# Row factors, low parts and attention's row sums moved from GpSimd to VectorE, and a longer written order in an MLP, in a two-layer decoder trunk

## The chip, the cores and the metric

The kernel runs on one core of a Trainium2 chip. A core has a matrix engine (TensorE, PE in the profile), a vector engine (VectorE, DVE), an engine for activation functions (ScalarE, ACT), a general engine (GpSimd, POOL) and a queue that issues transfers (SyncE, SP). They run side by side, each through its own list of instructions in order, and wait for each other by semaphores. The metric is the device time of one execution in microseconds; the median over the runs counts.

## The reference

A residual stream h of 1024 positions by 1024 channels, in float32, passes two layers. Each layer is a token mixer, an MLP and a gated embedding:

```python
h = h + rmsnorm(mixer(rmsnorm(h, g_mix_pre)), g_mix_post)
f = square(relu(rmsnorm(h, g_ffn_pre) @ w_up)) @ w_down          # 1024 -> 4096 -> 1024
h = h + rmsnorm(f, g_ffn_post)
e = sigmoid(rmsnorm(h, g_ple_pre) @ w_gate + b_gate) * (p[i] @ w_proj)
h = h + rmsnorm(e, g_ple_post)
```

with rmsnorm(x, g) = x * (mean(x^2) + 1e-6)^-0.5 * g. The first layer's mixer is a gated MLP over chunks of 128 positions. The second's is differential attention with eight heads: each head has two causal softmaxes over scores of width 64, and its rows are (softmax 1 - lambda * softmax 2) times values of width 128, followed by an RMS norm per head and an output projection.

## The kernel before

**Numbers in two parts.** A float32 operand is split into a high part, a copy rounded by ACT, and a low part, the difference, made by DVE or POOL. A product then takes three matmuls: high by high, high by low, low by high. `split` (line 111) does this for weights, line 114 being the subtraction; its argument `eng` says which engine subtracts. `WStream` loads blocks of weights in a written sequence and passes `nc.gpsimd` for those that were added with `pool=True`. `cut` is the same for activations.

**Tiles.** The 1024 positions are eight tiles (tt = 0 to 7) of 128 rows, with 1024 columns each. An RMS norm of a tile needs a factor per row: ACT squares the tile and sums each row, and `rstd_of` (line 240) makes the factor of it on POOL in two operations on a 128x1 column, a multiply-add (line 243) and a power with exponent -0.5 (line 244). After a mixer, an MLP or an embedding there is a post-norm: the row sum comes in two halves, DVE adds them (line 401 in `post_part`, line 838 in `whole`), `rstd_of` follows, then `residual` (line 344) adds the scaled tile to h, stores it, and where a product follows, `pre_norm` squares it again (328), makes a second factor with `rstd_of`, and scales it (330). `transpose_to` then queues transposes on PE (296) and the cut of the result (282, 283) for a moment that is counted in columns of matmuls. Eight tiles have their factors at the start and in the gated MLP's layer norm, eight tiles pass five pre-norms and six post-norms: 104 calls of `rstd_of`.

**Order.** The whole program is emitted in one sequence. PE keeps that sequence throughout. The other engines' order is set by a planner, from estimated durations and from what is ready, except inside a block marked as manual for them, where the instructions emitted inside keep their order among themselves; other instructions may still be put between these.

**The MLP's second product** has four groups (g = 0 to 3) of 16, 16, 16 and 8 steps, numbered m = 0 to 55. A step is 24 matmuls. `after(m)` loads operands of later steps (`load_down`, by the list `lead_l`), stores what earlier splits left over (`store`), and splits operands of steps two or three ahead (`split_down`, by `lead_s`; lines 528 and 771 to 772). At a group's last step `evict` adds the PSUM banks into the tiles (lines 824 to 826 for the third group). Behind the third group, tiles 0 to 3 are done and have their post-norm, residual and pre-norm while the fourth group runs; the weights of the gate (lines 119 and 120) and, by `resident`, the four operands of the embedding's projection are loaded and split meanwhile. A manual block for PE, SP, ACT and DVE begins ahead of step 0 and ends where m reaches `FREE` = 45, that is three steps ahead of the third group's end.

**Attention** runs over sixteen units: heads 0 to 7 with the first 512 rows, then heads 0 to 7 with the last 512. A unit has eight scores: two softmaxes times four row tiles. For each, PE makes the scores, DVE the row maximum (1138), ACT the exponential (1141). After the second softmax of a row tile t, DVE makes a factor (1145, 1146), and the two are combined in A. For t = 1 and 3 one fused operation does this on DVE (line 1149). For t = 0 and 2 the second softmax is scaled in place, by DVE (1152) or ACT (1154), and added by POOL (1155). Some scores later PE transposes A (1167), ACT and DVE cut it (1171, 1172), PE multiplies by the values (1179 to 1181); `norm` and `close` finish the head, and `close` splits the result, its low part being POOL's (line 1208). Between all this PE works on projections that are handed to it piece by piece (`FILL`): the rest of the values, and the output projection, whose weights `w_o` are loaded and split three times in four blocks, the first two times with POOL (line 114).

## Time and profile before

| what | value |
|---|---|
| median of 3 runs | 2371.8 us (2368.11 to 2376.4) |
| the profiled execution | 2373.36 us |
| its span, first to last instruction | 2371.7 us |
| PE busy | 2316.4 us, 98% |
| DVE busy | 1603.4 us, 68% |
| ACT busy | 1167.3 us, 49% |
| POOL busy | 235.7 us, 10%, 303 instructions |
| granted TensorE clock | 0.994 |

The profile lists for one execution what each engine did and when. A row of a group of instructions has the line of the code, the engine, the operation, the tiles written and read, the shapes and the count; behind the bar the time in which any of them ran, in us, the mean of one in ns, and the idle time of the engine just before them with what ended it. A row of the timeline begins with the start and the duration in us; the brackets hold the idle time before it and what it waited for. A row of busy times has the stretch, its length, then each engine's busy time with its count of instructions, the granted clock, and the share and rate of the transfers. PEld is the weight load, which runs beside PE. Matmuls overlap, so PE's single durations add up to more than its busy time.

### The profile page before, as it was taken

The page shows a single profiled execution, that of the slowest core. Times are in us where ns is not written, and L with a number is a line of the kernel's source. Part 1 is how long each engine was busy: PE and PEld are TensorE (multiplying, and loading weights), DVE is VectorE, ACT ScalarE, POOL GpSimd, SP SyncE. Part 2 cuts the span into 40 slices and gives each one's busy share as a digit, 9 for nine tenths or more (in the row PEclk, how much of TensorE's full clock was granted, in tenths as well). Part 3 has the DMA queues.
Part 4 walks back from the last instruction along what each step waited for, and adds up shares of the span by engine and source line. Part 5 has one row for each costly group of instructions (what it writes and reads, how often), then busy time and mean ns, then how long its engine had stood idle before and what let it go on. Part 6 is the DMA issues. An engine that isn't in the chain of part 4 may idle for free.

```text
span 2371.7 us, 30563 instructions
## 1 busy us (share of the span) xinstructions
PE 2316.4 (98%) x10748; PEld 1919.4 (81%) x10748; DVE 1603.4 (68%) x2492; ACT 1167.3 (49%) x2003; POOL 235.7 (10%) x303
## 2 busy tenths in 40 slices
PE   9999999999999998999999989999999999999898
PEld 7888888888888877888887878777888888887787
DVE  4733697777856965563435888878877785876654
ACT  6232575555533446462324766657555553544541
POOL 1100100000000022010001342321000000000410
PEclk9999999999999999999999999999999999999999
DMA  9111445445888975154445765554544577988433
GB/s 334 57 36 54 150 157 183 160 158 189 287 255 297 292 243 213 63 180 145 162 134 181 222 189 138 160 187 138 191 159 161 175 282 240 294 287 298 159 107 125
DMA packets 205035, 441.04 MB, mean 186 GB/s; under 512 B 21552, under 2 KB 56368, under 8 KB 204752
## 3 DMA queue, kind: packets, MB, share of 16 engines
q1 hardware_dynamic: 204448, 437.89, 55.5%
q8 instruction: 85, 1.39, 0.3%
q0 software_dynamic: 432, 1.19, 0.2%
q14 instruction: 70, 0.57, 0.1%
HBM read 310.02 MB, written 133.17 MB: 187 GB/s over the span
## 4 chain that ended last, share of the span: by engine, by line
PE 64%; DVE 4%; DMA 3%; ACT 2%; POOL 1%; issue 1%; SPq 0%; DVEq 0%; POOLq 0%; ACTq 0%
PE pm_c L356 5%; PE pm_c L357 5%; PE pm_c L358 5%; PE pb L368 5%; PE pb L357 4%; PE pm_a L368 4%; PE pb L356 4%; PE pb L358 4%; PE pm_a L356 4%; PE pm_a L357 4%; PE pm_a L358 4%; PE pm_c L368 3%; PE pt L357 2%; PE pt L356 2%; PE pt L358 2%; DMA raw<-in_w_o_dram 1%
## 5 line engine op out<-in xcount | busy, mean ns | idle before, releaser
L368 PE MATMUL pm_a<-w,xh 128*128 128x512 f32 x704 | 222.4, 394 | 2.7 <-ACT w L119 1.8
L368 PEld LDWEIGHTS pm_a<-w,xh 128*128 128x128 f32 x704 | 131.0, 188 | 30.4 <-ACT w L119 3.0
L368 PE MATMUL pb<-w,xh 128*128 128x512 f32 x416 | 135.6, 402 | 5.5 <-DVE gbc L1027 2.9
L527 ACT ACTIVATE w<-ma 128x512 fp32r<-128x512 f32 x130 | 82.3, 635 | 114.2 <-PE pm_a L357 40.4
L368 PE MATMUL pm_a<-w,xl 128*128 128x512 f32 x352 | 138.2, 393 | 0.0
L114 POOL TENSOR_TENSOR s<-s 128x1024 fp32r<-128x1024 f32 x8 | 19.8, 2486 | 1131.5 <-ACT s L113 570.3
L527 ACT ACTIVATE xh<-xl 128x1024 fp32r<-128x1024 f32 x72 | 75.2, 1053 | 80.4 <-DMA xl<-hid 71.4
L528 DVE TENSOR_TENSOR xl<-xl,xh 128x1024 fp32r<-128x1024 f32 x72 | 87.5, 1219 | 28.1 <-ACT xh L527 27.8
L357 PE MATMUL pm_a<-xl,w 128*128 128x512 f32 x260 | 101.3, 390 | 0.2 <-DVE xl L283 0.2
L356 PE MATMUL pm_a<-xh,w 128*128 128x512 f32 x260 | 101.4, 390 | 0.0
L358 PE MATMUL pm_a<-xh,w 128*128 128x512 f32 x260 | 101.2, 389 | 0.0
L243 POOL TENSOR_SCALAR small<-small 128x1 f32<-128x1 f32 x104 | 43.1, 414 | 530.1 <-DVE small L401 322.8
L368 PEld LDWEIGHTS pb<-w,xh 128*128 128x128 f32 x416 | 77.5, 191 | 20.1 <-DVE xn L398 3.4
L528 DVE TENSOR_TENSOR w<-ma,w 128x512 fp32r<-128x512 f32 x130 | 88.5, 682 | 0.0
L527 ACT ACTIVATE s<-s 128x1024 fp32r<-128x1024 f32 x56 | 58.8, 1053 | 54.9 <-DMA s<-hid 38.2
L368 PE MATMUL pb<-w,xl 128*128 128x512 f32 x208 | 83.4, 401 | 0.0
L528 DVE TENSOR_TENSOR s<-s 128x1024 fp32r<-128x1024 f32 x56 | 68.1, 1220 | 22.0 <-ACT s L527 21.8
L344 DVE SCALAR_TENSOR_TENSOR hin<-ma,small,hin 128x1024 f32<-128x1024 f32 (+1 forms) x45 | 56.5, 1257 | 37.6 <-DMA hin<-h 22.8
L356 PE MATMUL pb<-xh,w 128*128 128x512 f32 x204 | 79.7, 391 | 0.0
L358 PE MATMUL pb<-xh,w 128*128 128x512 f32 x204 | 79.4, 389 | 0.0
L357 PE MATMUL pb<-xl,w 128*128 128x512 f32 x204 | 79.4, 389 | 0.0
L368 PEld LDWEIGHTS pm_a<-w,xl 128*128 128x128 f32 x352 | 66.2, 188 | 12.9
(510 smaller groups left out, 7013.8 us busy)
## 6 DMA issues: line engine op xcount, KB each, us to landing
xl<-hid SPq DMA_DIRECT2D x56, 512.0 KB, 4.7
ma<-in_f_w_up_dram SPq DMA_DIRECT2D x48, 512.0 KB, 3.7
ma<-in_f_w_down_dram SPq DMA_DIRECT2D x92, 256.0 KB, 5.2
hid<-ma SPq DMA_DIRECT2D x80, 256.0 KB, 2.4
s<-hid SPq DMA_DIRECT2D x40, 512.0 KB, 5.1
h<-hin SPq DMA_DIRECT2D x36, 512.0 KB, 3.2
hin<-h SPq DMA_DIRECT2D x36, 512.0 KB, 4.2
hid<-xn SPq DMA_DIRECT2D x64, 256.0 KB, 2.5
```

Source lines behind the costliest of these rows:

```text
L114: (eng or nc.vector).tensor_tensor(out=lo, in0=raw, in1=f32(hi), op=ALU.subtract)
L243: nc.gpsimd.tensor_scalar(out=ss, in0=ss, scalar1=1.0 / n, scalar2=eps, op0=ALU.mult, op1=ALU.add)
L344: nc.vector.scalar_tensor_tensor(out=h[:, cs], in0=t_ap[:, cs], scalar=rs, in1=h[:, cs], op0=ALU.mult, op1=ALU.add)
L356: nc.tensor.matmul(ps, lhsT=lh, rhs=rh, start=start, stop=False)
L357: nc.tensor.matmul(ps, lhsT=lh, rhs=rl, start=False, stop=False)
L358: nc.tensor.matmul(ps, lhsT=ll, rhs=rh, start=False, stop=stop)
L368: nc.tensor.matmul(ps, lhsT=xs(l, kc, tt * P), rhs=r[:, cs], start=kc == 0 and k == 0, stop=kc == KC - 1 and k == 2)
L527: act(h, v, AF.Copy)
L528: vec(out=l, in0=v, in1=f32(h), op=sub)
```

## The change

For post-norms, ACT's Square takes the scale 1/32, so that the row sums come out divided by 1024. DVE's addition of the two halves becomes a fused one that adds epsilon as well, and POOL does the power alone (`post_rstd`). Pre-norms, the start and the layer norm keep both POOL operations. The low parts of the embedding's four operands, of w_o's first two passes and of each head's result are made by DVE. Attention's rows are combined by the fused DVE operation for all four row tiles; the scaling by DVE or ACT and POOL's addition go. In the MLP's second product the manual block ends at step 47, behind the third group's evictions and ahead of the post-norms, not ahead of step 45; and `after` no longer calls `store` a second time from step 45 on.

```diff
     def rstd_of(ss, n, eps):
-        k = ss.shape[1]
         nc.gpsimd.tensor_scalar(out=ss, in0=ss, scalar1=1.0 / n, scalar2=eps, op0=ALU.mult, op1=ALU.add)
-        nc.gpsimd.tensor_tensor(out=ss, in0=ss, in1=mhalf[:, :k], op=ALU.pow)
+        root_of(ss)
+
+    def root_of(x):
+        nc.gpsimd.tensor_tensor(out=x, in0=x, in1=mhalf[:, 0:1], op=ALU.pow)
+
+    ROOT = 1.0 / 32
+
+    def post_rstd(s):
+        nc.vector.scalar_tensor_tensor(out=s[:, 0:1], in0=s[:, 0:1], scalar=RMS_EPS, in1=s[:, 1:2],
+                                       op0=ALU.add, op1=ALU.add)
+        root_of(s[:, 0:1])
...
-        nc.scalar.activation(junk, src, AF.Square, accum_out=ssq[tt][:, cb:cb + 1])
+        nc.scalar.activation(junk, src, AF.Square, scale=ROOT, accum_out=ssq[tt][:, cb:cb + 1])
...
-            s = ssq[tt]
-            nc.vector.tensor_tensor(out=s[:, 0:1], in0=s[:, 0:1], in1=s[:, 1:2], op=ALU.add)
-            rstd_of(s[:, 0:1], D, RMS_EPS)
+            post_rstd(ssq[tt])
...
-        split(nc, f32(lo), hi, lo, eng=nc.gpsimd)
+        split(nc, f32(lo), hi, lo)
...
-        FREE = 3 * NQ - 3
...
-            if t >= FREE:
-                store()
...
         for m, (g, c) in enumerate(steps):
-            if m == FREE:
-                strict.__exit__(None, None, None)
...
             if c == n_c - 1 and g == 2:
+                strict.__exit__(None, None, None)
                 for p in range(4):
                     half(p, 1)
...
-                if t in STT[u.hf]:
-                    nc.vector.scalar_tensor_tensor(out=a_, in0=e, scalar=f, in1=a_, op0=ALU.mult, op1=ALU.add)
-                else:
-                    if t in TS[u.hf]:
-                        nc.vector.tensor_scalar(out=e, in0=e, scalar1=f, scalar2=None, op0=ALU.mult)
-                    else:
-                        nc.scalar.activation(e, e, AF.Copy, scale=f)
-                    nc.gpsimd.tensor_tensor(out=a_, in0=e, in1=a_, op=ALU.add)
+                nc.vector.scalar_tensor_tensor(out=a_, in0=e, scalar=f, in1=a_, op0=ALU.mult, op1=ALU.add)
...
-            nc.gpsimd.tensor_tensor(out=ol, in0=o, in1=f32(oh), op=ALU.subtract)
+            nc.vector.tensor_tensor(out=ol, in0=o, in1=f32(oh), op=ALU.subtract)
...
-                ws.add(a["w_o"][b, t], None, n < 2, slot=W_O[4 * n + t])
+                ws.add(a["w_o"][b, t], slot=W_O[4 * n + t])
```

`half` and `whole` in the MLP get the same two edits as `post_part`.

More of the change, by code (lines that the diff above doesn't have):

```diff
@@ L832, in half @@
             ssq[tt] = small2[:, tt, :]
-            act(xn[0][:, 0:512], m, AF.Square, accum_out=ssq[tt][:, cb:cb + 1])
+            act(xn[0][:, 0:512], m, AF.Square, scale=ROOT, accum_out=ssq[tt][:, cb:cb + 1])
             vec(out=m, in0=m, in1=cols(gbc, cb), op=ALU.mult)
         def whole(tt, us):
-            s = ssq[tt]
-            vec(out=s[:, 0:1], in0=s[:, 0:1], in1=s[:, 1:2], op=add)
-            rstd_of(s[:, 0:1], D, RMS_EPS)
-            residual(tt, MA[:, tt, :], s[:, 0:1], hsrc, hdst, us, h=rows.pop(tt))
+            post_rstd(ssq[tt])
+            residual(tt, MA[:, tt, :], ssq[tt][:, 0:1], hsrc, hdst, us, h=rows.pop(tt))
         rows, rowR = {}, Ring(hin + [bbc])
@@ L1002, in _trunk @@
     NORM, CLOSE = 1, 3
-    STT = (1, 3), (1, 3)
-    TS = (2,), (0, 2)
     TAIL = 6
```

## The prediction

> **What bounds the kernel now.** I read the page first, then the busy times by stage, then TensorE's waits, and last the timelines of the engines around the longest of them.
>
> ```profile
> span 2371.7 us, 30563 instructions
> PE 2316.4 (98%) x10748; PEld 1919.4 (81%) x10748; DVE 1603.4 (68%) x2492; ACT 1167.3 (49%) x2003; POOL 235.7 (10%) x303
> ```
>
> PE is at work for 2316.4 of 2371.7 us, in an order that is written by hand, and the change touches no matmul. All that it can win lies in the other 55.3 us. Where are they? The busy times of four stretches say (us, PE, PEld, DVE, ACT, POOL): attention, the ends of the two MLPs, and the tail.
>
> ```profile
> 1265.00:1580.00 315.00, 295.83 (x1648) 251.89 (x1646) 255.49 (x501) 202.38 (x458) 104.38 (x86) 0.98 0.64 185
> 850.00:930.00 80.00, 71.67 (x322) 58.29 (x321) 50.58 (x69) 43.66 (x72) 28.60 (x27) 0.98 0.57 212
> 2150.00:2240.00 90.00, 80.91 (x352) 65.24 (x351) 52.88 (x68) 45.35 (x67) 23.85 (x20) 0.96 0.71 251
> 2363.00:2371.70 8.70, 1.26 (x6) 0.72 (x4) 3.59 (x6) 1.35 (x3) 0.74 (x2) 0.81 0.22 86
> ```
>
> PE is idle 19.2 us in attention, 8.3 and 9.1 us where the MLPs end, 7.4 us in the tail: 44.0 of the 55.3 us. These are also the stretches where POOL works. In attention DVE is busy for 255.5 of 315 us, so 59.5 us of it are free; at the MLP ends 29.4 and 37.1 us are free. (DVE is VectorE, ACT ScalarE, POOL GpSimd, SP the DMA queue.)
>
> **The row factors.** Of 104 pairs of POOL operations (multiply-add on line 243, power on line 244), 48 lose the first: those behind the six post-norms of eight tiles. The factor 1/1024 goes into the Square that ACT does anyway, and the epsilon into the DVE addition that is there already (128x1), so neither engine gets an instruction more. In the tail, the pair stands alone:
>
> ```profile
> 2366.10 0.19 POOL L243 TENSOR_SCALAR small<-small 128x1 f32<-128x1 f32 x1 [5.97 <-DVE small L401]
> 2366.37 0.55 POOL L244 TENSOR_TENSOR small<-small,mhalf 128x1 f32<-128x1 f32 x1
> ```
>
> From start to start it is 0.27 us, and all later work hangs on it: **-0.3 us**. At an MLP's end the same operations are longer. This is POOL after the first MLP's third group, and then who waits for it:
>
> ```profile
> 878.77 1.77 POOL L243 TENSOR_SCALAR small<-small 128x1 f32<-128x1 f32 x1 [3.32 <-DVE small L838]
> 880.62 0.95 POOL L244 TENSOR_TENSOR small<-small,mhalf 128x1 f32<-128x1 f32 x1
> 881.65 2.56 POOL L243 TENSOR_SCALAR small<-small 128x1 f32<-128x1 f32 x1
> 884.30 3.21 POOL L244 TENSOR_TENSOR small<-small,mhalf 128x1 f32<-128x1 f32 x1
> 887.59 1.29 POOL L243 TENSOR_SCALAR small<-small 128x1 f32<-128x1 f32 x1
> ...
> 889.87 0.55 POOL L244 TENSOR_TENSOR small<-small,mhalf 128x1 f32<-128x1 f32 x1
> ```
>
> ```profile
> 890.45 1.15 ACT L330 ACTIVATE ma<-hin,small 128x1024 f32<-128x1024 f32 x1 [7.65 <-POOL small L244]
> ```
>
> ```profile
> 891.65 0.66 PE L296 MATMUL pt<-identr,ma 128*128 128x128 f32 x4 [2.22 <-ACT ma L330]
> 900.78 1.12 PE L296 MATMUL pt<-identr,ma 128*128 128x128 f32 x4 [3.88 <-DVE xl L283]
> 2217.41 0.66 PE L296 MATMUL pt<-identr,ma 128*128 128x128 f32 x4 [2.22 <-ACT ma L330]
> 2227.02 0.66 PE L296 MATMUL pt<-identr,ma 128*128 128x128 f32 x4 [2.76 <-DVE xl L283]
> ```
>
> Operations on one column take up to 3.21 us here, against 0.19 and 0.55 in the tail where DVE is idle. The last pair of this stretch is tile 0's pre-norm; behind it stand ACT's scaling (890.45), the transposes of tile 0 (891.65, 2.22 us late), and the fetch of a later row, whose buffer that scaling reads; the second wait, 3.88 us, follows on the same chain. Ahead of tile 0's pair stand three multiply-adds of post-norms, 1.77 + 2.56 + 1.29 = 5.6 us, which go. Not all of that is won: if they are long because DVE keeps POOL out, the power that follows inherits the block. Ends: 0 (the block only moves over) and 5.6 us; I take the middle, 2.8 us, since one of the two operations at each step stays and both kinds are seen long. The four waits hold 6.1 and 5.0 us, so a shift of 2.8 us fits into each: **-5.6 us** for both MLPs, bounds 0 and -10.6. Other post-norms I cost at nothing: matmuls run beside them.
>
> **The order at the third group's end.** The written order on DVE, ACT and SP now holds for three steps more (m = 45 to 47), up to the third group's evictions. The removed second call of store() is empty: the last append is made for step 47 behind t = 44, and the first call behind t = 45 empties the list. What does the order do to the evictions? Before, on DVE:
>
> ```profile
> 865.55 0.68 DVE L826 TENSOR_TENSOR ma<-pm_a,ma 128x512 f32<-128x512 f32 x1
> 866.15 1.22 DVE L528 TENSOR_TENSOR xl<-xl,xh 128x1024 fp32r<-128x1024 f32 x1
> 867.28 0.75 DVE L120 SCALAR_TENSOR_TENSOR w<-raw,gcol,w 128x512 fp32r<-128x512 f32 x1
> 867.95 0.68 DVE L825 TENSOR_TENSOR ma<-pb,ma 128x512 f32<-128x512 f32 x1
> ```
>
> The planner had set 824 and 826, which free the banks that the fourth group needs, ahead of 825, and put low parts of later work between them (528 and 120: 1.8 us from 866.15 to 867.95). PE waits there for line 826: 8.3 - 6.1 = 2.2 us in the first MLP and 9.1 - 5.0 = 4.1 us in the second. The written order brings all 825s forward, at most three more of them, 0.60 us from start to start, ahead of the last 826: up to +1.8 us each. If it also keeps those low parts out, the same 1.8 us go. They belong to later steps and may still be set in between, so between the waits' end (-2.2 and -4.1 us) on one side and +1.8 us each on the other I take **0**, bounds -6.3 and +3.6. On SP the three steps hold step 51's load, two stores and the fetch of row 2; behind them in that queue stand the PLE's weights and operands. On ACT and DVE they hold the splits of steps 48 and 49. Cost 0: loads are written three and more steps ahead of PE, splits three. If that cover were gone, PE would lose up to a step, 24 matmuls of 2316.4/10748 = 0.22 us, 5.2 us.
>
> **Low parts from POOL to DVE.** Eight splits of the PLE's operands (L114 on POOL) sit at the MLP ends. The second MLP shows what they do to DVE:
>
> ```profile
> 2193.71 5.17 POOL L114 TENSOR_TENSOR s<-s 128x1024 fp32r<-128x1024 f32 x2 [561.25 <-DMA s<-p]
> ```
>
> ```profile
> 2194.53 2.11 DVE L120 SCALAR_TENSOR_TENSOR w<-raw,gcol,w 128x512 fp32r<-128x512 f32 x1
> ```
>
> The form that took 0.75 us above takes 2.11 while POOL is in such an operation, and evictions that PE waits for stand behind it. That goes: 2.11 - 0.75, **-1.4 us**, and nothing if something else of DVE's takes its place there. On DVE the eight cost 1.22 us each (next fence), 4.9 us per MLP in 29 and 37 us of free time: 0, or +4.9 us each if every one lands ahead of what PE waits for.
>
> **Attention.** The rows for its sum (means; x8 is one per head):
>
> ```profile
> L1149 DVE SCALAR_TENSOR_TENSOR ma<-hin,small,ma 128x1024 f32<-128x1024 f32 x8 | 13.3, 1668 | 0.1
> L1149 DVE SCALAR_TENSOR_TENSOR ma<-hin,small,ma 128x768 f32<-128x768 f32 x8 | 12.1, 1515 | 0.1
> L1149 DVE SCALAR_TENSOR_TENSOR ma<-hin,small,ma 128x256 f32<-128x256 f32 x8 | 3.9, 488 | 0.0
> L1152 DVE TENSOR_SCALAR hin<-hin,small 128x896 f32<-128x896 f32 x8 | 8.3, 1042 | 0.4
> L1152 DVE TENSOR_SCALAR hin<-hin,small 128x384 f32<-128x384 f32 x8 | 5.2, 649 | 0.0
> L1152 DVE TENSOR_SCALAR hin<-hin,small 128x640 f32<-128x640 f32 x8 | 4.4, 549 | 0.4
> L114 DVE TENSOR_TENSOR w<-raw,w 128x1024 fp32r<-128x1024 f32 x4 | 4.9, 1223 | 5.4 <-ACT w L113 5.4
> ```
>
> ```profile
> L344 DVE SCALAR_TENSOR_TENSOR hin<-ma,small,hin 128x1024 f32<-128x1024 f32 x43 | 55.1, 1281 | 36.7 <-DMA hin<-h 22.8 <-POOL small L244 12.0 <-POOL xl L1208 1.2
> L528 DVE TENSOR_TENSOR w<-ma,w 128x512 fp32r<-128x512 f32 x130 | 88.5, 682 | 0.0
> ```
>
> The fused form without POOL beside it is L344: 1281 ns at 1024 columns; with 488 at 256, a line gives 1.03 ns per column: 0.36, 0.62, 0.88 and 1.15 us for 128, 384, 640 and 896 columns, eight each: +24.1 us. The scalings that go save 8.3 + 5.2 + 4.4 = 17.9. The 16 low parts in close() come from POOL at 0.68: +10.9; the eight splits of w_o at 1.22: +9.8. POOL's blocks go: 8 x (1668 - 1281) and 8 x (1515 - 1017 by the line) ns, -7.1. DVE gets **19.8 us more** and keeps 39.7 of its 59.5 free. What a block does to PE:
>
> ```profile
> 1379.64 3.22 DVE L1149 SCALAR_TENSOR_TENSOR ma<-hin,small,ma 128x768 f32<-128x768 f32 x1
> ```
>
> ```profile
> 1403.61 2.36 DVE L1149 SCALAR_TENSOR_TENSOR ma<-hin,small,ma 128x768 f32<-128x768 f32 x1
> ```
>
> ```profile
> 1384.45 0.38 PE L1181 MATMUL pb<-s,s 128*128 128x256 f32 x1 [2.22 <-DVE s L1172]
> 1406.62 0.80 PE L368 MATMUL pb<-w,xh 128*128 128x512 f32 x1 [2.87 <-DVE gbc L1027]
> ```
>
> The line gives 1.02 us for this form; blocked, it took 3.22 and 2.36, and the DVE operations queued behind it (low parts on 1172, an eviction on 1027) came late for PE, 2.22 and 2.87 us. These 5.1 us I take as the blocks' and gone. The other 19.2 - 5.1 = 14.1 us could grow as DVE's free time shrinks: in proportion (59.5/39.7) by 7.0 us, or not at all where the written lag of two or three scores between an exponential and its transposes covers DVE; I take half, +3.5. **-1.6 us**, bounds -19.2 (no wait left) and +19.8 (every added microsecond on the path).
>
> [...]
>
> **Sum.** -0.3 - 5.6 + 0 - 1.4 - 1.6 = -8.9 us. The profiled execution took 2373.4 us, its span and 1.7 around it, 1.6 above the median of 2371.8; the change taken off that median gives **2362.9**, off the profiled execution 2364.5.
>
> **Rivals.** *Hidden anyway* (2371): the blocks on POOL only move to the powers, DVE's new work eats what attention wins, the tail's 0.3 stays. For it: PE at 98%, and POOL at 10%. Against it: the waits at 891.65 and 2217.41 stand right behind POOL. *DVE becomes attention's bound* (slower): from about 1375 us on, row maxima, low parts and fused sums of all heads queue on one engine in order; if two thirds of the 19.8 us lengthen PE's waits and the relief is lost, that is +13, less some 5 at the MLP ends and the tail: 2380. It decides where DVE's free share there falls below about 5%; against it, 39.7 of 315 us, 13%, remain. *The blocks were behind most waits*: 10 of attention's 19.2 us go, and the full 10.6 at the MLP ends, with 1.7 for the tail and L120: -22.3, 2350. For it: the blocks add up to 7.1 us in two forms alone. Against it: the matmuls of attention wait on many different lines.
>
> **Chances.** Forecast (2358 to 2367) 0.45, hidden 0.25, DVE the bound 0.18, blocks behind most 0.12. No change means within 0.3%, 7.1 us, which is about what a measurement can tell here: 2364.7 to 2378.9. Three quarters of the forecast lie below that, 0.33; with the last rival, faster is 0.45. Same: 0.12 + 0.24 + 0.03 = 0.39. Slower: 0.15 + 0.01 = 0.16. The likeliest case's own range is 2358 to 2367; the whole, 2350 to 2378, leaves out about a tenth at each end.
>
> **What would show it.** Right: the multiply-add counted 56 times on POOL and not 104, POOL's operations between the third group's end and tile 0's scaling under 8 us, no wait of PE on L330, no fused sum over 1.3 us in attention, DVE busy there some 275 us. Wrong: PE's waits behind line 826 over 4 us per MLP (order), DVE over 95% in attention with waits on L1172 grown, or powers as long as pairs were.

## The result, and the profile after

The changed kernel takes 2392.7 us (median of six runs, 2391.36 to 2398.42), the kernel before 2373.5 us in six runs on the same chip. The ratio is 1.0084, with a 95% interval of 1.0069 to 1.0099: slower by 0.84%, some 20 us, where 2363 us was forecast and 2378 us was the upper end of the range. The time lies outside it, and on the other side.

In what follows the lines of the changed kernel are named by its own numbers: 824, 825 and 826 of before are 830, 831 and 832 now, the post-norm's multiplication 834 is 840, the fused addition of epsilon is 253, the POOL pair 243 and 244 is 242 and 247, the residual 344 is 355, a cut's subtraction 528 is 537, the prescaling 330 is 341, the transposes 296 are 307, their cut 283 is 294, and attention's fused sum 1149 is 1148.

The page of the changed kernel begins so:

```profile
span 2391.2 us, 30409 instructions
PE 2324.5 (97%) x10748; PEld 1923.9 (80%) x10748; DVE 1621.4 (68%) x2532; ACT 1164.2 (49%) x1995; POOL 116.9 (5%) x191
```

The span grew by 19.5 us, from 2371.7. PE is busy 8.1 us longer with the same 10,748 matmuls, and idle 66.7 us, not 55.3. POOL lost half of its work, 118.8 us, as intended. The busy times of the three stretches that the prediction showed (us, PE, PEld, DVE, ACT, POOL, clock; shifted by what the kernel is late there):

```profile
1275.00:1590.00 315.00, 291.74 (x1620) 246.88 (x1621) 265.21 (x529) 196.34 (x444) 21.57 (x25) 0.98 0.62 180
850.00:930.00 80.00, 65.77 (x280) 52.71 (x279) 45.71 (x60) 38.58 (x59) 10.81 (x12) 0.89 0.58 203
2165.00:2255.00 90.00, 74.91 (x316) 60.19 (x315) 53.28 (x67) 44.12 (x65) 10.70 (x12) 0.91 0.70 234
```

At the MLP ends PE now issues 280 matmuls in the 80 us in which it issued 322, and 316 for 352; the granted clock there fell from 0.98 and 0.96 to 0.89 and 0.91. Attention lost a little, 1620 for 1648. Since every kernel here issues the same matmuls in the same order (one experiment adds some, which are left out of the count), the time between two of them can be compared. This table is worked out from the starts in the traces, for the stretches that began in the kernel before at 866.7 us (first MLP's end, the first matmul of its fourth group, to 960), 1250 (attention, to 1590), 1590 (the mixer's end, to 1700) and 2187 (second MLP's end, to 2290). All other stretches differ by under 0.4 us, but for the program's start (up to 2 us).

| kernel | first MLP's end | attention | mixer's end | second MLP's end |
|---|---|---|---|---|
| before | 93.4 | 340.1 | 109.9 | 103.1 |
| changed | 102.9 | 345.7 | 107.6 | 110.4 |

So +9.5, +5.6, -2.3 and +7.3 us: together 20.1 us, of which the program's start and the tail give some 0.5 back, as the span grew by 19.5. The loss is in two kinds of places, the MLP ends and attention, that have nothing in common but the engine that got the work.

**The MLP ends.** The groups of PE's waits (total, times, longest), first two of before, then three of the changed kernel:

```profile
PE pm_c L356 <- DVE ma L826: 3.9, 3, 1.9
PE pm_a L356 <- DVE ma L826: 2.2, 2, 1.6
```

```profile
PE pm_a L367 <- DVE ma L832: 11.4, 3, 6.0
PE pm_c L367 <- DVE ma L832: 10.7, 3, 5.5
PE pt L307 <- DVE xl L294: 7.7, 3, 4.3
```

The waits behind tile 0's prescaling are gone, as forecast; those on the cut of the transposes (294, 283 before), which the prediction set on the same chain, stay, 7.7 us for 7.3; those on the evictions of the third group, which free the banks for the fourth, went from 6.1 to 22.1 us. PE's timeline in the first MLP of the changed kernel shows three of them, for the second, third and fourth tile's bank:

```profile
869.76 0.50 PE L367 MATMUL pm_a<-s 128*128 128x512 f32 x1 [1.72 <-DVE ma L832]
875.18 0.50 PE L367 MATMUL pm_a<-s 128*128 128x512 f32 x1 [3.76 <-DVE ma L832]
883.56 0.79 PE L367 MATMUL pm_a<-s 128*128 128x512 f32 x1 [5.95 <-DVE ma L832]
```

What DVE did meanwhile, first in the kernel before, then in the changed one:

```profile
869.15 0.68 DVE L826 TENSOR_TENSOR ma<-pm_a,ma 128x512 f32<-128x512 f32 x1
869.75 1.14 DVE L120 SCALAR_TENSOR_TENSOR w<-raw,gcol,w 128x512 fp32r<-128x512 f32 x1
870.80 0.68 DVE L824 TENSOR_TENSOR ma<-pm_a,ma 128x512 f32<-128x512 f32 x1
871.41 0.67 DVE L826 TENSOR_TENSOR ma<-pm_a,ma 128x512 f32<-128x512 f32 x1
...
872.60 0.67 DVE L826 TENSOR_TENSOR ma<-pm_a,ma 128x512 f32<-128x512 f32 x1
873.20 0.67 DVE L825 TENSOR_TENSOR ma<-pb,ma 128x512 f32<-128x512 f32 x1
```

```profile
869.03 0.68 DVE L832 TENSOR_TENSOR ma<-pm_a,ma 128x512 f32<-128x512 f32 x1
869.63 0.68 DVE L830 TENSOR_TENSOR ma<-pm_a,ma 128x512 f32<-128x512 f32 x1
870.23 0.68 DVE L840 TENSOR_TENSOR ma<-ma,gbc 128x512 f32<-128x512 f32 x1
...
870.89 2.35 DVE L114 TENSOR_TENSOR s<-s 128x1024 fp32r<-128x1024 f32 x2
...
873.85 0.68 DVE L831 TENSOR_TENSOR ma<-pt,ma 128x512 f32<-128x512 f32 x1
874.45 0.67 DVE L832 TENSOR_TENSOR ma<-pm_a,ma 128x512 f32<-128x512 f32 x1
875.05 0.67 DVE L830 TENSOR_TENSOR ma<-pm_a,ma 128x512 f32<-128x512 f32 x1
875.64 1.27 DVE L355 SCALAR_TENSOR_TENSOR hin<-ma,small,hin 128x1024 f32<-128x1024 f32 x1
876.84 2.35 DVE L537 TENSOR_TENSOR xl<-xl,xh 128x1024 fp32r<-128x1024 f32 x2
879.11 1.27 DVE L355 SCALAR_TENSOR_TENSOR hin<-ma,small,hin 128x1024 f32<-128x1024 f32 x1
880.31 1.40 DVE L120 SCALAR_TENSOR_TENSOR w<-raw,gcol,w 128x512 fp32r<-128x512 f32 x2
...
882.23 0.68 DVE L831 TENSOR_TENSOR ma<-pt,ma 128x512 f32<-128x512 f32 x1
882.83 0.67 DVE L832 TENSOR_TENSOR ma<-pm_a,ma 128x512 f32<-128x512 f32 x1
```

Before, DVE ran all four tiles' 824 and 826 by 873.3 us and kept three of the four 825, whose banks nobody needs soon, for last. Now each 832 stands behind the 831 of its tile, as the text of `evict` has them (830, 831, 832), and each 831 but the first is put off: ahead of it go the embedding's low parts (114), post-norms (840), residual rows (355) and later splits (537, 120). The last bank is free at 883.5 us, 10 us later than before. DVE is hardly idle in this time; it works in an order in which PE's needs come late.

**The tail** came as forecast: the addition starts 0.82 us ahead of the residual, not 1.10 (2365.85 to 2366.95 before), with this one operation of POOL between:

```profile
2385.95 0.55 POOL L247 TENSOR_TENSOR small<-small,mhalf 128x1 f32<-128x1 f32 x1 [6.25 <-DVE small L253]
```

### The profile page after: what moved, and what is told of

It reads as the page before. It is cut to its first block, busy times and chain, and to the rows that moved or that the text cites. A ratio compares the mean times of both kernels' runs of the same rounds, so it can differ in the third digit from the quotient of the medians.

```text
span 2391.2 us, 30409 instructions
## 1 busy us (share of the span) xinstructions
PE 2324.5 (97%) x10748; PEld 1923.9 (80%) x10748; DVE 1621.4 (68%) x2532; ACT 1164.2 (49%) x1995; POOL 116.9 (5%) x191
## 4 chain that ended last, share of the span: by engine, by line
PE 64%; DVE 5%; DMA 3%; ACT 1%; issue 1%; SPq 0%; POOL 0%; DVEq 0%; POOLq 0%; ACTq 0%
PE pm_c L367 5%; PE pm_c L369 5%; PE pm_c L368 5%; PE pb L379 5%; PE pb L369 4%; PE pb L367 4%; PE pb L368 4%; PE pm_a L367 4%; PE pm_a L379 4%; PE pm_a L368 4%; PE pm_a L369 4%; PE pm_c L379 3%; PE pt L367 2%; PE pt L368 2%; PE pt L369 2%; PE pt L307 1%
## 5 line engine op out<-in xcount | busy, mean ns | idle before, releaser
L247 POOL TENSOR_TENSOR small<-small,mhalf 128x1 f32<-128x1 f32 x104 | 75.9, 732 | 1588.5 <-DVE small L253 1583.8
L536 ACT ACTIVATE xh<-xl 128x1024 fp32r<-128x1024 f32 x72 | 75.4, 1053 | 95.7 <-DMA xl<-hid 73.6
L379 PEld LDWEIGHTS pm_a<-w,xl 128*128 128x128 f32 x352 | 66.7, 190 | 13.2
L1138 DVE TENSOR_REDUCE small<-pm_b 128x1 f32<-128x640 f32 (+1 forms) x64 | 65.1, 1018 | 13.8 <-PE pm_b L1137 13.6
L1164 ACT ACTIVATE s<-pt 128x512 fp32r<-128x512 f32 (+1 forms) x96 | 47.0, 490 | 53.4 <-PE pt L1160 52.5
```

Of the source, the lines that this page charges most:

```text
L247: nc.gpsimd.tensor_tensor(out=x, in0=x, in1=mhalf[:, 0:1], op=ALU.pow)
L379: nc.tensor.matmul(ps, lhsT=xs(l, kc, tt * P), rhs=r[:, cs], start=kc == 0 and k == 0, stop=kc == KC - 1 and k == 2)
L536: act(h, v, AF.Copy)
L1138: nc.vector.tensor_reduce(out=u.nm[:, j], in_=S[:, 0:nk], axis=AX.X, op=ALU.max, negate=True)
L1164: nc.scalar.activation(ah, pt[:, r], AF.Copy)
```

## The experiments

Two questions: which parts make the loss at the MLP ends, and which piece costs in attention. The number of an experiment is that of its label. All ratios are to the kernel before, run on the same chip, with 95% intervals. The expectations call the embedding PLE, and their line 826 is 832 in the kernels that come from the changed one. The table has the times between the same matmuls, as above.

| experiment | ratio | first MLP's end | attention | mixer's end | second MLP's end |
|---|---|---|---|---|---|
| 1: changed, block to 45 | 0.9970 [0.9958, 0.9982] | 90.4 | 346.6 | 107.9 | 98.5 |
| 2: before, block to the group's end | 1.0002 [0.9991, 1.0014] | 94.8 | 339.5 | 112.3 | 100.5 |
| 3: changed, block to 47 | 0.9959 [0.9945, 0.9973] | 89.4 | 345.6 | 107.8 | 94.8 |
| 4: before, attention's part | 1.0033 [1.0021, 1.0044] | 94.3 | 347.6 | 110.3 | 100.4 |
| 5: 3 with attention as before | 0.9934 [0.9920, 0.9949] | 89.0 | 341.7 | 107.7 | 94.9 |
| 6: changed, embedding's low parts on POOL | 0.9995 [0.9985, 1.0005] | 93.7 | 347.5 | 107.5 | 101.1 |
| 7: before, row factors alone | 0.9968 [0.9955, 0.9981] | 92.8 | 340.4 | 106.9 | 98.6 |
| 8: changed, PE kept busy | 1.0074 [1.0057, 1.0091] | 100.3 | 345.1 | 108.0 | 111.3 |
| 9: 5 with the fused sums | 0.9925 [0.9910, 0.9939] | 88.8 | 338.9 | 106.8 | 96.4 |
| 10: 5 with attention's low parts on DVE | 0.9955 [0.9941, 0.9969] | 87.8 | 344.9 | 107.8 | 95.7 |
| 11: changed, banks first | 0.9941 [0.9924, 0.9959] | 89.0 | 350.6 | 106.8 | 93.9 |
| 12: 11 and 9 together | 0.9916 [0.9902, 0.9929] | 90.4 | 338.0 | 106.8 | 93.5 |
| 13: 9 with the heads' low parts on DVE | 0.9948 [0.9934, 0.9962] | 87.7 | 338.4 | 107.5 | 96.9 |
| 14: 9 with w_o's low parts on DVE | 0.9955 [0.9943, 0.9968] | 89.5 | 340.5 | 106.8 | 99.3 |

Each cell comes from one execution. Where the code of a stretch is the same, the cells still differ: attention takes 345.1 to 347.6 us in the changed kernel and the experiments 1, 3, 4, 6 and 8, and 350.6 in 11; the second MLP's end 94.8 to 99.3 in 3, 5, 9, 10, 13 and 14. A difference of 2 or 3 us in one cell says little by itself.

**1. The order undone.** The changed kernel, with the manual block ending ahead of step 45 as before:

```diff
         for m, (g, c) in enumerate(steps):
+            if m == 45:
+                strict.__exit__(None, None, None)
...
-                strict.__exit__(None, None, None)
```

> The changed kernel with the manual block ending ahead of step 45 again; all of the change's work that moved from POOL to DVE stays. Theory A (the third group's evictions: in the written order 826 of a tile may not pass 825 of the same tile, which the planner sets late, so the banks of the fourth group come free late): PE's waits behind 826 fall back to 2 to 4 us per MLP, TensorE's clock is not halved for 13.65 us there, and the time is 2362 to 2374. Theory B (DVE has too much work since POOL's came to it): the time stays near 2390, since all of that work is still there.

2368.1 us, 0.9970: 1.1% below the changed kernel. With the block's old end the rest of the change gains, so the longer order takes part in the loss.

**2. The order alone.** The kernel before, with the block to the group's end and nothing else:

```diff
-            if m == FREE:
-                strict.__exit__(None, None, None)
...
             if c == n_c - 1 and g == 2:
+                strict.__exit__(None, None, None)
```

> The kernel before with the longer manual block alone; POOL keeps all its operations. Theory A: PE waits behind 826 some 7 to 11 us per MLP, the clock is halved behind it, and the time is 2383 to 2393. Theory B: within 7 us of the kernel before, 2366 to 2380.

2374.3 us, 1.0002: no change, where theory A had 2383 to 2393. The waits on the third group's evictions did grow, to 7.4 us in the first MLP, the longest of them in PE's timeline (823 is 826 of before):

```profile
877.56 0.80 PE L356 MATMUL pm_a<-s 128*128 128x512 f32 x1 [4.99 <-DVE ma L823]
```

But the four waits of the transposes, 11.1 us in the kernel before, vanished in exchange. The order alone is not the cause; it must meet another part.

**3. The block to step 47.** The changed kernel, with the block ending at the head of step 47, so that the evictions are free again:

```diff
         for m, (g, c) in enumerate(steps):
+            if m == 47:
+                strict.__exit__(None, None, None)
...
-                strict.__exit__(None, None, None)
```

> The changed kernel with the manual block ending at the head of step 47: the written order holds for the loads, stores and splits of steps 45 and 46, but no longer for the evictions. Theory A (the evictions alone): as with the block ending ahead of step 45, 2362 to 2376, waits behind 826 under 5 us per MLP. Theory C (the order of the loads and splits of steps 45 and 46, above all on SP and ACT, delays later steps): 2383 to 2393, with the waits behind splits or transfers and not behind 826.

2364.1 us, 0.9959, and only two short waits on the evictions in the first MLP, 0.63 us and this one:

```profile
872.52 0.50 PE L367 MATMUL pm_a<-s 128*128 128x512 f32 x1 [0.87 <-DVE ma L832]
```

Steps 45 and 46 in written order cost nothing; all of the harm is in the evictions of step 47.

**4. Attention alone.** The kernel before, with the fused sums for all tiles and the low parts of the heads and w_o on DVE:

```diff
-                if t in STT[u.hf]:
-                    nc.vector.scalar_tensor_tensor(out=a_, in0=e, scalar=f, in1=a_, op0=ALU.mult, op1=ALU.add)
-                else:
...
+                nc.vector.scalar_tensor_tensor(out=a_, in0=e, scalar=f, in1=a_, op0=ALU.mult, op1=ALU.add)
...
-            nc.gpsimd.tensor_tensor(out=ol, in0=o, in1=f32(oh), op=ALU.subtract)
+            nc.vector.tensor_tensor(out=ol, in0=o, in1=f32(oh), op=ALU.subtract)
...
-                ws.add(a["w_o"][b, t], None, n < 2, slot=W_O[4 * n + t])
+                ws.add(a["w_o"][b, t], slot=W_O[4 * n + t])
```

> The kernel before with the attention part of the change alone: fused row sums for all tiles, the low parts of the heads and of w_o by DVE. The forecast's sum gives -1.6 us for it. With the order undone PE waited 22.8 us in attention (12.6 to 15.9 hundred us) against 19.3 before, so theory D (DVE's added work costs more than POOL's blocks gave back) says +2 to +6 us, 2376 to 2382. Theory E (the blocks' end pays for it, and what was seen comes from the other edits): 2370 to 2375.

2384.3 us, 1.0033: slower by 0.2 to 0.4%, somewhat more than either theory had, and 7.5 us in the stretch itself (340.1 to 347.6). A second loss, which needs neither the order nor the embedding's low parts.

**5. Attention as before**, in the kernel of the third experiment: the same edit the other way round.

> The changed kernel with the manual block ending at the head of step 47 and attention as before (row sums of two tiles, the heads' and w_o's low parts on POOL); row factors and the PLE's low parts stay changed. Theory D: 2357 to 2363, faster than the same block with the new attention (2364). Theory E: 2364 to 2368.

2359.8 us, 0.9934, 6 us below the third experiment's ratio, 3.9 us of it in the stretch. It beats both kernels.

**6. The embedding's low parts back on POOL**, in the changed kernel with its long block:

```diff
-        split(nc, f32(lo), hi, lo)
+        split(nc, f32(lo), hi, lo, eng=nc.gpsimd)
```

> The changed kernel with the low parts of the PLE's four operands (line 114 at the MLP ends) back on POOL; the long manual block stays. Theory F (the written order is harmful because those low parts and residual sums now stand on DVE between 825 and 826 of the third and fourth tile): they no longer stand there, PE's waits behind 826 fall from 11 to some 7 to 8 us per MLP, the clock is halved for some 10 us and not 13.65, 2378 to 2386. Rival (the low parts play no part; the powers alone change the planner's order): 2389 to 2395.

2373.9 us, 0.9995, below the 2378 to 2386 that theory F had: some 21 us of the changed kernel's time go with eight subtractions. POOL's and DVE's timelines in the first MLP:

```profile
868.75 5.15 POOL L114 TENSOR_TENSOR s<-s 128x1024 fp32r<-128x1024 f32 x2 [563.14 <-ACT s L113]
```

```profile
869.66 2.03 DVE L840 TENSOR_TENSOR ma<-ma,gbc 128x512 f32<-128x512 f32 x1
871.62 2.30 DVE L253 SCALAR_TENSOR_TENSOR small<-small 128x1 f32<-128x1 f32 x1
```

The low parts cost DVE time there too: beside POOL's subtractions the fused addition lasts 2.30 us, a form that takes 0.15 behind them (874.45). But the third and the fourth tile's banks then come at 875.8 and 879.4 us, not at 875.2 and 883.5, since ahead of the last 831 (878.12) DVE has 1.8 us of other work behind the tile's 830, not 6.6; PE's timeline shows it:

```profile
875.85 0.79 PE L367 MATMUL pm_a<-s 128*128 128x512 f32 x1 [4.99 <-DVE ma L832]
...
879.45 0.51 PE L367 MATMUL pm_a<-s 128*128 128x512 f32 x1 [0.67 <-DVE ma L832]
```

Together with the first and the second experiment: the embedding's low parts on DVE are worth about -0.3% where the block ends at 45 (0.9970, against 0.9968 x 1.0033 = 1.0001 for the product of row factors and attention, which was not run as one kernel), and cost 0.9% under the long block (1.0084 against 0.9995). The two parts are harmless or good one by one and bad together. The gain is the less sure of the two: it stands on a product of ratios, and at the MLP ends the profiled executions of the first and the seventh experiment differ by 2.5 us, not 7.

**7. The row factors alone.** The kernel before, with `post_rstd`, the Square's scale 1/32 and the power alone on POOL, as in the change's diff, and nothing else.

> Before plus the row factors' part alone: the 1/1024 in the Square, the epsilon in the addition, the power alone on POOL; the order's end, the PLE's low parts and attention are as before. If the prediction's term is right, 2.8 us go at each MLP's end and 0.3 in the tail: 2367 to 2369 beside 2373 to 2375. If the blocks on POOL only move over to the powers, 0.3 us: 2373 to 2375, and the waits behind tile 0's scaling stay near 2.2 us. In either case no wait behind line 826's successor grows, since nothing of the order is changed.

2367.3 us, 0.9968: 7.6 us (4.5 to 10.7) less, at the side where the prediction's term holds. By place, 0.6 and 4.5 us at the MLP ends, and 3.0 at the mixer's end; against the fourth experiment, where these places are as before too, 1.5, 1.8 and 3.4.

**8. PE kept busy.** The changed kernel, with matmuls whose results are thrown away, ahead of the third and the fourth tile's first matmul of step 48:

```diff
+                    if g == 3 and c == 0 and e == 0:
+                        for _ in range((0, 0, 14, 22)[p]):
+                            nc.tensor.matmul(PB[0], lhsT=hh[:, 0:P], rhs=wh[:, 0:512], start=True, stop=True)
```

> The changed kernel with 14 and 22 matmuls more on PE, into a bank that nobody reads then, where PE waits for the third and fourth tile's 826; their results are thrown away. VectorE's order is unchanged. If the halved clock (13.65 us from 875.8 us on and again in the second MLP) is the answer to PE's idling, the clock stays at 1.00 there and the time falls by some 6 to 13 us, to 2380 to 2387, though PE has 72 matmuls more to do. If the clock is halved for another reason, the halved stretches stay and the time stays at 2390 or grows.

The question was whether the halved clock behind these waits (last section) makes part of the loss. PE's timeline (869 are the matmuls thrown away):

```profile
870.02 3.36 PE L869 MATMUL pb<-s 128*128 128x512 f32 x14
...
875.44 5.15 PE L869 MATMUL pb<-s 128*128 128x512 f32 x22
882.33 0.50 PE L367 MATMUL pm_a<-s 128*128 128x512 f32 x1 [1.74 <-DVE ma L832]
```

The clock stays whole there (the matmuls behind both waits start 0.23 us apart, not 0.43; the run's mean granted clock is 0.995, for 0.989), and the time hardly moves: 2391.7 us, 1.0074, inside the interval of the changed kernel, and not the 2380 to 2387 expected if the halved clock made part of the loss. The first MLP's end takes 100.3 us, not 102.9; in the second the stretch is 111.3 us, not 110.4: what the clock gives back is waited for later, at the transposes (6.4 us, not 4.3). DVE's chain sets the end; of the clock, some 2 us at most are seen at the two ends together.

**9 and 10. Attention's two pieces**, each alone in the kernel of the fifth experiment: the fused sums for all tiles (9), the low parts of the heads and w_o on DVE (10); the edits are the first, and the second and third, of the fourth experiment.

> The kernel of the fifth experiment (order to step 47, attention as before: 2359.8 us) with attention's fused sums for all tiles on DVE as in the changed kernel, and the low parts of the heads and of w_o left on POOL. Theory D1 (attention's loss comes from the fused sums: a tile's sum is due right ahead of the transposes that read it, and each now stands in DVE's line ahead of the next operation): 2363 to 2365, nearly all of the 4.3 us between the third and the fifth experiment. Theory D2 (it comes from the low parts, which DVE must now write before the mixer's products can start): 2359 to 2361. In both POOL is nearly out of attention's first part.

> The kernel of the fifth experiment with only the low parts of the heads and of w_o on DVE; the sums of attention's rows as before, with ACT and POOL. Theory D1 (the fused sums cost): 2359 to 2361. Theory D2 (the low parts cost): 2363 to 2365. If the two pieces only hurt together, both this and the ninth experiment stay near 2360.

The fused sums: 2356.6 us, 0.9925, no loss (D1 had 2363 to 2365, D2 2359 to 2361), and in the stretch 2.8 us less than the fifth (338.9 for 341.7). The low parts: 2365.0 us, 0.9955, and 344.9. From the ninth to the third experiment, which has both pieces, it is 0.34%, 8 us, with intervals that do not overlap. Next to the fused sums, the low parts are the cost, and PE's idle time in the stretch shows it: 18.5 us in the ninth, 23.9 in the third. Without the fused sums the time points the same way (0.9955 for 0.9934, intervals that overlap), but the tenth's profiled execution has PE no more idle than the fifth's (18.7 for 20.1 us); it has more work at half clock (20.5 us for 13.7; granted clock 0.97 for 0.98 from 1265 to 1580 us). How the low parts cost there is open.

**11. Banks first.** The changed kernel, with its long block, but the four 831 emitted behind all 830 and 832 of the step:

```diff
             elif g == 2:
                 vec(out=m22, in0=a_, in1=m12, op=add)
-                vec(out=m12, in0=b_, in1=m12, op=add)
                 vec(out=m21, in0=a_, in1=m21, op=add)
...
             if c == n_c - 1 and g == 2:
+                for p in range(4):
+                    m12 = cols(MA[:, p], 1)
+                    vec(out=m12, in0=other[p], in1=m12, op=add)
                 strict.__exit__(None, None, None)
```

> The changed kernel, with its order written to the third group's end as it is, but with the four evictions that the fourth group's first banks don't need (825 of before) emitted behind the eight that it does need (824 and 826), in the same step. Theory (the loss at the MLP ends comes from 826 being tied behind 825, whose late due time it inherits, so that the PLE's low parts and the row work of other tiles are set in front of it): the waits of 3.8 and 5.5 to 6.0 us of the fourth group's first matmuls shrink to some 1 to 2 us, the clock is not halved for 13.65 us, and the time is 2365 to 2374. Rival (the block's later end itself does it, by holding ACT and SP): the waits stay, 2388 to 2394.

2360.3 us, 0.9941: 1.4%, or 34 us, below the changed kernel, by the place of four instructions of 0.68 us per MLP, and below the 2365 to 2374 expected. DVE, in which 831 is now the old 826 and 882 the old 825:

```profile
869.24 0.68 DVE L831 TENSOR_TENSOR ma<-pm_a,ma 128x512 f32<-128x512 f32 x1
869.84 1.22 DVE L114 TENSOR_TENSOR s<-s 128x1024 fp32r<-128x1024 f32 x1
...
871.58 0.68 DVE L831 TENSOR_TENSOR ma<-pm_a,ma 128x512 f32<-128x512 f32 x1
872.17 1.28 DVE L882 TENSOR_TENSOR ma<-pb,ma 128x512 f32<-128x512 f32 x2
```

and PE's one wait on these evictions:

```profile
872.31 0.50 PE L367 MATMUL pm_a<-s 128*128 128x512 f32 x1 [0.70 <-DVE ma L831]
```

The long block and the low parts on DVE are both still in this kernel. What is gone is the tie of the bank-freeing evictions to the late ones. A low part (114) still gets between, but only one, and the last bank is free at 872.3 us. PE's waits on tile 0's prescaling (341) are back, 6.4 us in the two MLPs together, but the MLP ends are 13.9 and 16.5 us shorter than in the changed kernel. The rival, that the block's later end itself does harm by holding ACT and SP, falls.

**12. The gaining pieces together**: the eleventh's order, and the low parts of the heads and w_o back on POOL.

> The pieces that gained, together: the changed kernel with the four evictions of 825 emitted behind the eight that free banks (as in the eleventh experiment), and the low parts of the heads and of w_o back on POOL (as in the ninth). If the two pieces are worth what they were alone (the eleventh: 2360.3 with the low parts on VectorE; the ninth: some 3 us below the fifth, the low parts some 5 to 8 us): 2353 to 2357, and below both kernels. If the low parts only cost where the order is cut at step 47: 2359 to 2361.

2350.7 us (2349.78 to 2354.66), 0.9916, a little below what was expected if the two add up: faster than before by 0.7 to 1.0%, and 1.7% below the changed kernel. Attention takes 338.0 us, the MLP ends 90.4 and 93.5.

**13 and 14. Which low parts.** The ninth experiment with the heads' low parts on DVE (13) or w_o's (14).

> The ninth experiment's kernel (2356.6 us) with only the low parts of the heads (16 of 128x512, 10.9 us of work on VectorE) moved to VectorE. The third experiment's kernel, which differs from the ninth by these and by w_o's, took 2364.1. Theory H (the heads' low parts cost, because they are set among the row maxima that the next scores' exponentials wait for): 2360 to 2364. Theory W (w_o's cost): 2356 to 2358. In proportion to their work (10.9 of 20.7 us): about 2360.5, with the fourteenth at the same.

> The ninth experiment's kernel (2356.6 us) with only the low parts of w_o (eight of 128x1024, 9.8 us of work on VectorE) moved to VectorE. Theory H (the heads' low parts cost): 2356 to 2358. Theory W (w_o's cost, 1.22 us each in one piece ahead of a row maximum or an eviction): 2360 to 2364. In proportion: about 2360.

2358.1 us (0.9948) and 2361.0 us (0.9955), against 0.9925 with neither and 0.9959 with both: each seems to cost something, 0.2 and 0.3%, and both together less than the sum of the two; the intervals do not tell the two theories apart, and neither holds alone. The traces say more. This is the wait of A's transposes on the fused sums, in the changed kernel, the ninth and the fourteenth experiment (whose lines are one further on):

```profile
PE pt L1160 <- DVE ma L1148: 3.9, 4, 1.7
```

```profile
PE pt L1161 <- DVE ma L1149: 0.6, 1, 0.6
```

```profile
PE pt L1161 <- DVE ma L1149: 3.8, 3, 2.0
```

With w_o's low parts on DVE the sums come late for PE, 3.8 us as with both; with the heads' it is 1.6 us. In all, PE is idle in the stretch for 18.5 us with neither, 19.8 with the heads', 21.7 with w_o's and 23.9 with both (third experiment). So the extra work shows up as late sums, though the sums are not the extra work. That the 1.22 us of one of w_o's subtractions, in one piece ahead of a sum, does more than the 0.68 us of a head's is likely from this, not shown.

## Why the prediction was wrong, point by point

**The written order, "0, bounds -6.3 and +3.6".** This is the step that failed, and with it the sum. Alone the order is worth what the prediction said: 1.0002 in the second experiment. In the change it met the low parts, and PE's waits on the evictions went from 6.1 to 22.1 us; with the 831 emitted last (eleventh experiment) they are 1.4 us, and the time is 34 us lower. But the reason given, that "the written order brings all 825s forward, at most three more of them, 0.60 us from start to start, ahead of the last 826", took for granted that the pair moves to the earlier place. It moved to the later one: 831 was put off, 832 of the same tile and 830 of the next had to come behind it, and whatever the planner set ahead of 831 now stood ahead of the banks that PE needs. The text of the kernel before said that other instructions may be put between those of a block; the prediction used that for the low parts it saw there (528 and 120) and not for the evictions themselves. The price of a tie is not the length of the tied instruction, 0.60 us, but the time for which that instruction is put off: 3.6 us for the third tile's 831 (other work from 870.23 to 873.85) and 6.6 for the fourth's (875.64 to 882.23).

**The embedding's low parts, "-1.4" in place of POOL's block, and "0, or +4.9 us each if every one lands ahead of what PE waits for".** The second half was the right question, with bounds costed for this part alone. Under the long block two of the four in each MLP did land there (870.89, 2.35 us), and the eight cost 21 us (sixth experiment), more than twice the 9.8 of the bound, since the chain of evictions then waits through the other tiles' rows as well. With the block's old end they are worth some -7 us by the product of the other parts' ratios, which no run measured alone, against the 1.4 forecast. That the parts were summed as if each met the kernel before is the second half of the failed step: the fourth and the seventh experiment and the second multiply to 1.0003, and the sixth, which has just these three parts, measured 0.9995; only the fourth part does not add up.

**Attention, "-1.6".** Wrong in sign: +7.8 us alone (fourth experiment). The price of the fused form was right within 1%, 0.88 and 1.15 us forecast for 640 and 896 columns, and none went over 1.3 us:

```profile
L1148 DVE SCALAR_TENSOR_TENSOR ma<-hin,small,ma 128x896 f32<-128x896 f32 x8 | 9.1, 1141 | 0.0
L1148 DVE SCALAR_TENSOR_TENSOR ma<-hin,small,ma 128x640 f32<-128x640 f32 x8 | 7.0, 880 | 0.1
```

The added work was over-sized: DVE is busy 265.2 of 315 us where 275 were forecast, and between the same matmuls of the stretch 275.5 us, 11.5 more than before (264.0) and not 19.8. The term that failed is the growth of the waits, "+3.5" as half of a proportion, against a relief of 5.1. Of the relief 1.2 to 2.8 us came, with the fused sums (the ninth experiment's stretch is 1.2 us under that of before, and 2.8 under the fifth's); the low parts then took 6.7 us in the stretch (338.9 to 345.6, ninth to third). The free share of DVE stayed at 16%, far from the 5% of the second rival, *DVE becomes attention's bound*; the rival's mechanism (work queued on one engine in order) fits PE's waits, without the engine being full: 3.9 us on the fused sums, which were not there before, and 5.4 for 4.2 on the cut's subtraction (1172, now 1165).

**The row factors, "-5.6" and "-0.3".** Right: 7.6 us measured alone (4.5 to 10.7) against 5.9. Place by place it was less exact: 0.6 and 4.5 us at the MLP ends where 2.8 each were forecast, and 3.0 at the mixer's end, which was costed at nothing because matmuls run beside its post-norms. In the first MLP the blocks largely moved over, as the lower bound had it. These are POOL's rows of the seventh experiment, three powers and then tile 0's own multiply-add, which took 0.19 us in the kernel before:

```profile
879.80 5.21 POOL L247 TENSOR_TENSOR small<-small,mhalf 128x1 f32<-128x1 f32 x3 [3.59 <-DVE small L253]
885.09 3.09 POOL L242 TENSOR_SCALAR small<-small 128x1 f32<-128x1 f32 x1
```

In the changed kernel it shows in POOL's groups, 732 ns for a mean power against 650 before and 0.55 us in the tail:

```profile
L247 POOL TENSOR_TENSOR small<-small,mhalf 128x1 f32<-128x1 f32 x104 | 75.9, 732 | 1588.5 <-DVE small L253 1583.8
L242 POOL TENSOR_SCALAR small<-small 128x1 f32<-128x1 f32 x56 | 18.9, 338 | 180.4 <-ACT ma L339 104.4 <-DVE small L442 38.4 <-ACT xn L1397 37.5
```

**What was to show it.** 56 multiply-adds; POOL's operations ahead of tile 0's scaling 6.3 us; no wait of PE on the prescaling; no fused sum over 1.3 us: as forecast. "PE's waits behind line 826 over 4 us per MLP" was named as what would prove it wrong: 11.4 and 10.7 us. *Hidden anyway* falls, since the row factors alone gained more than the tail; *the blocks were behind most waits* falls too, since between the same matmuls of attention PE is idle for 23.6 us in the changed kernel, with most of POOL's work gone, and for 18.5 in the ninth experiment, against 19.5 before.

The +20 us, part by part against the kernel before: row factors -7.6, attention +7.8, order 0, and some +20 for the embedding's low parts as they meet the order. No case of the prediction had the last.

## What to carry to other kernels

Where a written order takes in instructions that somebody waits for together with instructions that nobody waits for, each gets the lateness of the other: before fixing an order, ask of every instruction in it how long it may be put off, and emit those that free a buffer ahead of those that do not. When a change has several parts on one engine, cost them in pairs too: a part that fills that engine's line is free only as long as nothing that others need is tied behind it. And an engine at 81 to 84%, as DVE in attention here, can already be late: what counts is what stands in line ahead of the next thing somebody waits for, not the free share.

## What the runs showed of the hardware

Behind the long waits PE ran at half its clock. Busy times of the same 13.6 us, in the changed kernel and in the kernel before (clock in the third column from the end):

```profile
875.80:889.40 13.60, 7.65 (x19) 5.48 (x18) 11.42 (x16) 7.82 (x17) 5.31 (x6) 0.50 0.48 161
```

```profile
875.80:889.40 13.60, 13.60 (x61) 10.95 (x59) 12.58 (x17) 6.62 (x16) 10.21 (x6) 1.00 0.28 112
```

The halved clock lasts 13.65 us in each MLP, and begins in the first at 875.8 us, just behind waits of 1.72 and 3.76 us; matmuls of 0.23 us from start to start take 0.43 there. In the changed kernel 51.1 us of the span were at half clock (mean granted clock 0.989), in the kernel before 27.2 (0.994). Most of PE's 8.1 us of longer work fits this: in the pieces at half clock 91 matmuls started in the changed kernel, and PE was busy for 33.4 us, in the kernel before 68 and 22.6 us. At 0.23 us each they would have taken an estimated 20.9 and 15.6 us, so the halved clock makes 12.5 and 7.0 us, 5.5 us of the difference.

In these two traces the pieces at half clock last 3.41 us or two, three or four times that (6.83, 10.24, 13.65), but for the one that the program's end cuts off, and they start whole multiples of 3.41 us apart. In the 3.41 us ahead of 875.8 PE still worked for 0.60 us. Cut into stretches of 3.41 us from these starts, behind the first matmul, both kernels have 2.0 to 3.4 us of PE's idle time in each stretch ahead of a halving, and at most 1.78 us in any other stretch at full clock. The eighth experiment adds that the halved clock cost little of its own here, since PE would have waited instead: the two MLP ends together took 211.6 us with the clock whole behind these waits, and 213.3 with it halved.

In the sixth experiment, beside POOL's two subtractions (128x1024, 5.15 us together from 868.75 on), DVE's multiplication of two SBUF tiles (840) took 2.03 us and the fused addition on one column (253) 2.30; behind them the same two took 0.68 and 0.15 (873.85 and 874.45). An eviction with one operand in PSUM, beside the same subtractions, kept its 0.68 us (830 at 869.06). That the operand in PSUM is what spared it is the author's reading; no run changes that alone.
